# Down projection of a hybrid encoder block: PSUM banks from standing pools, another order of the pairs, and a block-wise end of the first column group

## The chip, the cores and the metric

One core of a Trainium2 chip runs the whole layer as one program. The metric is the device time of one execution in microseconds (us); runs of one kernel are compared by their median. TensorE (PE) does the matrix products, VectorE (DVE) and ScalarE (ACT) the elementwise work, SyncE (SP) issues the transfers.

## The reference, cut to what matters

A residual block on 256 tokens of width 2048 in float32: a normed input projection, eight heads of chunked attention and eight of a gated recurrence, an output projection, then the gated feed-forward part and a last norm. The change lies in the last product and what hangs on it:

```python
h2 = rmsnorm(x, norm2_gain[l])
ff = jax.nn.silu(h2 @ w_gate[l]) * (h2 @ w_up[l])      # 256 x 5632
x = x + (ff @ w_down[l]).astype(x.dtype)               # 5632 x 2048
return rmsnorm(x, final_gain)
```

## The kernel before, in words

**Split products.** Every float32 operand is split into a high and a low part (`split`, L86 to L88: ACT copies the rounded high part `wh`, DVE subtracts it from the source and gets `wl`), and a product is three matmuls: high by high, high by low, low by high. The weights stream through: `load_chunk` (L133) fetches 1 MB into one of three `raw` buffers, `halves_of` (L697) splits up to 1024 columns at a time into one of four `wh` and four `wl` buffers (`wsp`, L49).

**Gate and up.** The loop at L659 makes 22 blocks of 256 hidden columns. Each takes two banks of the pool `pacc` (four banks, tag `acc`) for the gate and two for the up product (`tr_product`, L159). `tr_evac` (L175) empties them: an ACT copy (L178), a DVE add that is the bank's last reader (L179), a DVE multiply (L180). The product of the two becomes `fh` and `fl`, the split hidden activations.

**Down.** The 5632 rows of `w_down` are 22 pairs of two 128-row blocks, the 2048 columns are two groups (g = 0, 1) of two 512-column halves. A group holds eight PSUM banks from the first product to the last: `c00`, `c01`, `c10`, `c11` (token half t, column half h) and `m1`, `m5`, `m6`, `m7`. A pair is done in one of two ways. *Ordinary* (`plain`, kind "d"): eight block products, 24 matmuls, for which DVE makes two 1024-column splits. *Seven-product* (`fast`, kind "s"): a Strassen-like scheme with seven block products, 21 matmuls, for which DVE makes three extra differences of the weights (`ta`, `tb`, L735 to L737) and splits 3.5 times 1024 columns. The seven-product pairs need sums of the activations, `sf`, made by four calls of `row_sums` (L679), each for two pairs. When the last seven-product pair of a group is done, `spread` (L767) adds the `m` banks into the residual `x2`; when the group is done, `add_res` (L782) adds the `c` banks, ACT takes the squares (L787), and DVE multiplies by the final gain (L788).

**Order of the work.** The lists `first` and `second` (L819 to L826) give the items in their order. Group 0: ordinary pairs 8 to 11, then pairs 0 to 7 as seven-product pairs, each followed by an ordinary one, then two ordinary ones: 8 seven-product and 14 ordinary pairs, 504 matmuls. Group 1 starts with a seven-product pair, has 504 matmuls too, and its last two pairs are kept (`tail`) and multiplied bank by bank, so that the closing norm (`finish`, L790) of one token half runs beside the products of the other. `row_sums` is called after items 1 to 4, `load_fg` (1 MB, the broadcast gain) after item 5. The banks of the down part come from a pool of their own, `pdn` (L675), opened after `pacc` and `paux` were closed (L668, L669). The scheduler of the framework keeps the program's dependencies but may place an engine's instructions a little earlier or later than they are written.

Of the kernel before, what the change touches and what calls it, by code (L numbers as in the profile page):

```python
# [8 lines left out]
F32 = mybir.dt.float32  # L9
# [19 lines left out]
FAST = 8  # L29
NT4 = 10  # L30
# [12 lines left out]
def hybrid_block(ctx: ExitStack, tc: tile.TileContext, x, xT, w_in, w_out, w_gu, w_down,  # L43
# [624 lines left out]
    auxs.__exit__(None, None, None)  # L668
    accs.__exit__(None, None, None)  # L669
# [5 lines left out]
    pdn = ctx.enter_context(tc.tile_pool(name="pdn", bufs=1, space=PSUM))  # L675
# [38 lines left out]
    class Group:  # L714
        def __init__(self, g, items):
            self.g, self.items = g, items
            self.bank = {n: pdn.tile([P, W], F32, tag=n, name=n) for n in
                         ("c00", "c01", "c10", "c11", "m1", "m5", "m6", "m7")}
            ns = sum(1 for kind, _ in items if kind == "s")
            nd = len(items) - ns  # L720
            self.left = {n: 3 * (ns + 2 * nd) if n in ("c00", "c01", "c10") else
                         6 * nd if n == "c11" else 3 * ns for n in self.bank}
            self.total = dict(self.left)

        def mul(self, n, lhs, rhs):
            for a, b in ((lhs[0], rhs[0]), (lhs[0], rhs[1]), (lhs[1], rhs[0])):
                nc.tensor.matmul(self.bank[n], lhsT=a, rhs=b, start=self.left[n] == self.total[n],  # L727
                                 stop=self.left[n] == 1)
                self.left[n] -= 1

        def fast(self, j):
            raw = load_pair(self.g, j)
            ta = dn.tile([P, 2, W], F32, tag="ta", name="ta")
            tb = dn.tile([P, 2, W], F32, tag="tb", name="tb")
            nc.vector.tensor_tensor(ta, raw[:, 1:3], raw[:, 0:2], ALU.subtract)  # L735
            nc.vector.tensor_tensor(tb[:, 0], raw[:, 2], ta[:, 0], ALU.subtract)
            nc.vector.tensor_tensor(tb[:, 1], raw[:, 3], tb[:, 0], ALU.subtract)  # L737
            b11, = halves_of(raw[:, 0:1])
            self.mul("m1", f_of(2 * j, 0), b11)
            t1, t3 = halves_of(ta)  # L740
            self.mul("m5", s_of(j, 0), t1)
            self.mul("m7", s_of(j, 2), t3)
            b22, b21 = halves_of(raw[:, 2:4])
            self.mul("c01", s_of(j, 3), b22)
            self.mul("c00", f_of(2 * j + 1, 0), b21)
            t2, t4_ = halves_of(tb)
            self.mul("m6", s_of(j, 1), t2)
            self.mul("c10", f_of(2 * j + 1, 1), t4_)

        def plain(self, j):  # L750
            raw = load_pair(self.g, j)
            out_ = []
# [5 lines left out]
        def plain_mul(self, steps, t=None, h=None):  # L758
            for k, hh, w in steps:
                for tt in range(NT):  # L760
                    if (t is None or tt == t) and (h is None or hh == h):
                        self.mul(f"c{tt}{hh}", f_of(k, tt), w)
# [19 lines left out]
    def add_res(gr, t, h):  # L782
# [4 lines left out]
        nc.scalar.activation(jk, x2[:, t, cols], AF.Square, accum_out=ss3[:, t, slot:slot + 1])  # L787
        nc.vector.tensor_tensor(x2[:, t, cols], x2[:, t, cols], fg[:, cols], ALU.mult)  # L788
# [28 lines left out]

    slow = list(range(FAST, KP))
    first = [("d", j) for j in slow[0:4]]  # L819
    later = slow[4:-2]  # L820
    second = []
    for i in range(FAST):
        first += [("s", i)] + [("d", j) for j in later[i:i + 1]]
        second += [("s", i)] + [("d", j) for j in slow[i:i + 1]]
    first += [("d", j) for j in slow[-2:]]
    second += [("d", j) for j in slow[FAST:]]  # L826
    sums = list(range(FAST // 2))
    for g, items in enumerate((first, second)):
        gr = Group(g, items)
        n_fast, tail = 0, []  # L830
        for n, (kind, j) in enumerate(items):
            if kind == "s":
                gr.fast(j)
                n_fast += 1
                if n_fast == FAST:
                    gr.spread()
            elif g == 1 and n >= len(items) - 2:
                tail += gr.plain(j)
            else:
                gr.plain_mul(gr.plain(j))  # L840
            if g == 0 and sums and (n >= 1):
                row_sums(sums.pop(0))
            if g == 0 and n == 5:
                load_fg()
        if g == 0:
            for t, h in ((0, 1), (0, 0), (1, 0), (1, 1)):
                add_res(gr, t, h)
        else:
            for t in range(NT):
                for h in range(2):  # L850
                    gr.plain_mul(tail, t, h)
                    if h == 0:
                        add_res(gr, t, h)
                finish(gr.bank[f"c{t}1"], t)
# [59 lines left out]
```

## Time and profile before

| | |
|---|---|
| three runs | 1174.12, 1174.25, 1175.63 us (median 1174.25) |
| the profiled execution | 1173.68 us, of which the span from first to last instruction is 1171.6 us |
| busy, share of the span | PE 99%, weight loads (PEld) 84%, DVE 70%, ACT 53% |
| down part, first and last matmul start | 928.94 and 1162.36 us |
| matmuls in the down part | 1008 |
| granted TensorE clock, mean | 0.998 |

How to read it: a row of a timeline is a start, a duration, the engine, the line, the operation, output<-inputs, and in brackets how long the engine had been idle and what ended that. A matmul's duration (0.39 us here) overlaps the next one's, so the spacing of starts, not the duration, is what a matmul costs in a stream. In the chain of waits a row gives start, length, and how many matmuls were merged (x27). A few records of matmuls are missing, so counts are taken from the code and not from the rows.

### The profile page before, as it was taken

The page shows a single profiled execution, that of the slowest core. Times are in us where ns is not written, and L with a number is a line of the kernel's source. Part 1 is how long each engine was busy: PE and PEld are TensorE (multiplying, and loading weights), DVE is VectorE, ACT ScalarE, POOL GpSimd, SP SyncE. Part 2 cuts the span into 40 slices and gives each one's busy share as a digit, 9 for nine tenths or more (in the row PEclk, how much of TensorE's full clock was granted, in tenths as well). Part 3 has the DMA queues.
Part 4 walks back from the last instruction along what each step waited for, and adds up shares of the span by engine and source line. Part 5 has one row for each costly group of instructions (what it writes and reads, how often), then busy time and mean ns, then how long its engine had stood idle before and what let it go on. Part 6 is the DMA issues. An engine that isn't in the chain of part 4 may idle for free.

```text
span 1171.6 us, 15526 instructions
## 1 busy us (share of the span) xinstructions
PE 1155.2 (99%) x6118; PEld 987.7 (84%) x6118; DVE 819.5 (70%) x1097; ACT 625.4 (53%) x858; POOL 19.1 (2%) x33
## 2 busy tenths in 40 slices
PE   9999999999999999999999999999999999999996
PEld 7888888888888888888888888888888777878885
DVE  7577778858646556666666657666666798899875
ACT  7465556747554455544445444444444455555543
POOL 3300000000000000000000000000000000000000
PEclk9999999999999999999999999999999999999999
DMA  8655454554745555555555555555555455656661
GB/s 313 240 206 193 145 180 168 193 179 146 279 151 180 180 180 180 185 204 187 182 193 201 180 185 200 191 180 193 201 182 184 175 181 214 216 180 216 212 219 72
DMA packets 35064, 223.85 MB, mean 191 GB/s; under 512 B 4144, under 2 KB 4656, under 8 KB 9520
## 3 DMA queue, kind: packets, MB, share of 16 engines
q1 hardware_dynamic: 34992, 222.87, 54.2%
q8 instruction: 48, 0.79, 0.3%
q14 instruction: 24, 0.20, 0.0%
HBM read 220.75 MB, written 2.10 MB: 190 GB/s over the span
## 4 chain that ended last, share of the span: by engine, by line
PE 93%; DVE 3%; DMA 1%; ACT 1%; issue 1%; SPq 0%; ACTq 0%; DVEq 0%
PE acc L168 38%; PE acc L170 19%; PE c L727 13%; PE acc L143 5%; PE acc L145 5%; PE acc L144 5%; PE m L727 3%; DVE wl L88 1%; PE vps L144 1%; PE vps L143 1%; PE vps L145 1%; DMA raw<-in_w_down_dram 1%; ACT wh L87 1%; DMA xr<-in_xT_dram 0%; PE pa L532 0%
## 5 line engine op out<-in xcount | busy, mean ns | idle before, releaser
L88 DVE TENSOR_TENSOR wl<-raw,wh 128x1024 fp32r<-128x1024 f32 (+1 forms) x418 | 492.8, 1184 | 276.6 <-ACT wh L87 271.7
L87 ACT ACTIVATE wh<-raw 128x1024 fp32r<-128x1024 f32 (+1 forms) x418 | 425.3, 1022 | 363.2 <-PE acc L168 215.5
L168 PE MATMUL acc<-h,wh 128*128 128x512 f32 x1408 | 488.6, 394 | 0.0
L170 PE MATMUL acc<-h,wl 128*128 128x256 f32 x1408 | 390.1, 277 | 0.0
L168 PEld LDWEIGHTS acc<-h,wh 128*128 128x128 f32 x1408 | 264.0, 188 | 61.4
L170 PEld LDWEIGHTS acc<-h,wl 128*128 128x128 f32 x1408 | 264.2, 188 | 0.0
L168 PE MATMUL acc<-hx,wh 128*128 128x512 f32 x512 | 179.7, 395 | 0.0
L170 PE MATMUL acc<-hx,wl 128*128 128x256 f32 x512 | 142.9, 279 | 0.0
L168 PEld LDWEIGHTS acc<-hx,wh 128*128 128x128 f32 x512 | 96.0, 187 | 21.5
L727 PE MATMUL c<-wh,fh 128*128 128x512 f32 x256 | 99.2, 391 | 3.1 <-DVE tb L179 2.7
L727 PE MATMUL c<-wl,fh 128*128 128x512 f32 x256 | 99.8, 390 | 0.1
L727 PE MATMUL c<-wh,fl 128*128 128x512 f32 x256 | 99.7, 389 | 0.0
L170 PEld LDWEIGHTS acc<-hx,wl 128*128 128x128 f32 x512 | 96.5, 189 | 0.1
L178 ACT COPY tb<-acc 128x256 f32<-128x256 f32 x120 | 43.3, 364 | 78.5 <-PE acc L170 78.5
L179 DVE TENSOR_TENSOR tb<-acc,tb 128x256 f32<-128x256 f32 x120 | 50.1, 421 | 30.3 <-ACT tb L178 30.3
L727 PEld LDWEIGHTS c<-wh,fh 128*128 128x128 f32 x256 | 47.9, 188 | 14.1 <-DVE tb L179 3.0
L727 PEld LDWEIGHTS c<-wl,fh 128*128 128x128 f32 x256 | 48.1, 188 | 10.9 <-DVE wl L88 0.9
L727 PEld LDWEIGHTS c<-wh,fl 128*128 128x128 f32 x256 | 48.1, 188 | 9.9
L143 PE MATMUL acc<-wh,hx 128*128 128x512 f32 x128 | 50.4, 394 | 0.0
L145 PE MATMUL acc<-wh,hx 128*128 128x512 f32 x128 | 49.9, 390 | 0.0
L144 PE MATMUL acc<-wl,hx 128*128 128x512 f32 x128 | 49.9, 389 | 0.0
L727 PE MATMUL m<-wh,sf 128*128 128x512 f32 x96 | 34.9, 391 | 0.6 <-ACT wh L87 0.6
(254 smaller groups left out, 1135.5 us busy)
## 6 DMA issues: line engine op xcount, KB each, us to landing
raw<-in_w_gu_dram SPq DMA_DIRECT2D x88, 1024.0 KB, 4.8
raw<-in_w_in_dram SPq DMA_DIRECT2D x48, 1024.0 KB, 4.9
raw<-in_w_down_dram SPq DMA_DIRECT2D x44, 1024.0 KB, 4.8
raw<-in_w_out_dram SPq DMA_DIRECT2D x16, 1024.0 KB, 4.8
raw<-in_w_in_dram SPq DMA_DIRECT2D x12, 512.0 KB, 6.7
raw<-in_w_in_dram SPq DMA_DIRECT2D x8, 256.0 KB, 5.0
x<-in_x_dram SPq DMA_DIRECT2D x2, 1024.0 KB, 9.3
out_dram<-x SPq DMA_DIRECT2D x8, 256.0 KB, 2.6
```

The lines of the kernel that those rows point to most:

```text
L87: nc.scalar.activation(hi, src, AF.Copy)
L88: nc.vector.tensor_tensor(lo, src, hi.bitcast(F32), ALU.subtract)
L143: nc.tensor.matmul(ps[t], lhsT=xh[:, tok], rhs=wh, start=kt == 0, stop=False)
L144: nc.tensor.matmul(ps[t], lhsT=xh[:, tok], rhs=wl, start=False, stop=False)
L145: nc.tensor.matmul(ps[t], lhsT=xl[:, tok], rhs=wh, start=False, stop=kt == kts - 1)
L168: nc.tensor.matmul(ps[m].rearrange("p j t -> p (j t)"), lhsT=wh[:, col], rhs=both, start=kt == 0, stop=False)
L170: nc.tensor.matmul(ps[m][:, 0, :], lhsT=wl[:, col], rhs=rhs[:, kt, 0, :], start=False, stop=kt == KD - 1)
L178: nc.scalar.copy(tb, ps[m][:, 1, :])
L179: nc.vector.tensor_tensor(tb, ps[m][:, 0, :], tb, ALU.add)
L727: nc.tensor.matmul(self.bank[n], lhsT=a, rhs=b, start=self.left[n] == self.total[n], stop=self.left[n] == 1)
```

## The change

Three things change, all in the down part.

1. **Banks.** `pacc` and `paux` stay open to the end. A group takes its eight banks from them, at its first product (`open`): the `c` banks in turn from `pacc`, the `m` banks from `paux`. The pool `pdn` is gone.
2. **Order and mix.** `order_of(fast, lead)` writes the lists. Group 0 now begins with six ordinary pairs (7 to 12) and has seven seven-product pairs (0 to 6); pair 7 becomes an ordinary one. Group 1 keeps eight, behind one ordinary pair. An ordinary pair now runs in the order c00, c01, c10, c11.
3. **Preparing and the group boundary.** `fast` and `plain` only load and split, and return their products as a list of steps; one loop over both groups prepares the next item and then multiplies. At the last pair of group 0 (`edge`) the first pair of group 1 is prepared first; the last pair is then multiplied bank by bank, `add_res` after each bank, and the four multiplications by the gain (`gained`) come after all of them.

The core of the diff:

```diff
-    accs = tc.tile_pool(name="pacc", bufs=4, space=PSUM)
-    pacc = accs.__enter__()
-    auxs = tc.tile_pool(name="paux", bufs=4, space=PSUM)
-    paux = auxs.__enter__()
+    pacc = ctx.enter_context(tc.tile_pool(name="pacc", bufs=4, space=PSUM))
+    paux = ctx.enter_context(tc.tile_pool(name="paux", bufs=4, space=PSUM))
...
-    auxs.__exit__(None, None, None)
-    accs.__exit__(None, None, None)
...
-    pdn = ctx.enter_context(tc.tile_pool(name="pdn", bufs=1, space=PSUM))
...
-            self.bank = {n: pdn.tile([P, W], F32, tag=n, name=n) for n in
-                         ("c00", "c01", "c10", "c11", "m1", "m5", "m6", "m7")}
+            self.bank = {}
...
+        def open(self):
+            for n in BANKS:
+                pool, tag = (pacc, "acc") if n[0] == "c" else (paux, "aux")
+                self.bank[n] = pool.tile([P, W], F32, tag=tag, name=n)
+
         def mul(self, n, lhs, rhs):
+            if not self.bank:
+                self.open()
...
-                out_ += [(2 * j + k, h if k == 0 else 1 - h, parts[h]) for h in range(2)]
-            return out_
+                steps += [(f"c{t}{h}", f_of(2 * j + k, t), parts[h if k == 0 else 1 - h])
+                          for t in range(NT) for h in range(2)]
+            return steps
...
+        def run_blocks(self, steps, blocks, after):
+            for t, h in blocks:
+                self.run([st for st in steps if st[0] == f"c{t}{h}"])
+                after(t, h)
...
+    def gained(gr, t, h):
+        cols = gr.cols(h)
         nc.vector.tensor_tensor(x2[:, t, cols], x2[:, t, cols], fg[:, cols], ALU.mult)
...
-    first = [("d", j) for j in slow[0:4]]
...
+    def order_of(fast, lead):
+        slow = [j for j in range(KP) if j not in fast]
+        items = [("d", j) for j in slow[:lead]]
+        mid = slow[lead:-2]
+        for n, j in enumerate(fast):
+            items += [("s", j)] + [("d", k) for k in mid[n:n + 1]]
+        return items + [("d", k) for k in mid[len(fast):]] + [("d", j) for j in slow[-2:]]
+
+    groups = [Group(0, order_of(list(range(FAST - 1)), 6))]
...
+    second = order_of(list(range(FAST)), 1)
...
-            for t, h in ((0, 1), (0, 0), (1, 0), (1, 1)):
-                add_res(gr, t, h)
...
+        if n == edge:
+            now, steps = steps, prepare(*todo[n + 1])
+            order = ((0, 0), (0, 1), (1, 0), (1, 1))
+            groups[0].run_blocks(now, order, lambda t, h: add_res(groups[0], t, h))
+            for t, h in order:
+                gained(groups[0], t, h)
+            continue
...
+        if n + 1 < len(todo):
+            steps = prepare(*todo[n + 1])
+    groups[1].run_blocks(held, ((0, 0), (0, 1), (1, 0), (1, 1)), last_block)
```

What this moves on the engines, at three places. Names carry a running number; the banks' names are those above, and all line numbers past the first lines shift (the matmul of `mul` is L727 before and L729 after).

**PE, first matmuls of the down part.** Before: the first rows; what stands in brackets are the engines or queues whose signals the instruction waits for.

```order
L727 MATMUL c00_8148<-wh_8158,fh_3829 128x512 [waits DMAHW4_49,DMAHW6_49,DMAHW2_49,DVE_49]
L727 MATMUL c00_8148<-wl_8159,fh_3829 128x512
L727 MATMUL c00_8148<-wh_8158,fl_3830 128x512
L727 MATMUL c10_8150<-wh_8158,fh_3829 128x512
L727 MATMUL c10_8150<-wl_8159,fh_3829 128x512
L727 MATMUL c10_8150<-wh_8158,fl_3830 128x512
L727 MATMUL c01_8149<-wh_8158,fh_3829 128x512
L727 MATMUL c01_8149<-wl_8159,fh_3829 128x512
L727 MATMUL c01_8149<-wh_8158,fl_3830 128x512
L727 MATMUL c11_8151<-wh_8158,fh_3829 128x512
```

After, from the fourth matmul on (three on `c00` from `wh_8145`, the first of which waits for ACT and the second for DVE, stand ahead of these):

```order
L729 MATMUL c01_8154<-wh_8145,fh_3829 128x512 [waits PE_49]
L729 MATMUL c01_8154<-wl_8146,fh_3829 128x512
L729 MATMUL c01_8154<-wh_8145,fl_3830 128x512
L729 MATMUL c10_8155<-wh_8145,fh_3829 128x512 [waits DVE_49]
L729 MATMUL c10_8155<-wl_8146,fh_3829 128x512
L729 MATMUL c10_8155<-wh_8145,fl_3830 128x512
L729 MATMUL c00_8153<-wh_8149,fh_3829 128x512
L729 MATMUL c00_8153<-wl_8150,fh_3829 128x512
L729 MATMUL c00_8153<-wh_8149,fl_3830 128x512
L729 MATMUL c11_8156<-wh_8145,fh_3829 128x512 [waits DVE_49]
L729 MATMUL c11_8156<-wl_8146,fh_3829 128x512
L729 MATMUL c11_8156<-wh_8145,fl_3830 128x512
```

Before, the first matmul on `c00` is the one that waits for DVE's reading of the old banks; after, the waits for DVE stand at the first matmul on `c10` and on `c11`, and `c11` has become the 13th matmul.

**DVE, around the first seven-product pair of group 0** (`a`, `sm`, `sf` are of `row_sums`; `ta`, `tb` of the seven-product pair). Before:

```order
L689 TENSOR_TENSOR sm_8311<-a_8310,sm_8311 128x256
L735 TENSOR_TENSOR ta_8321<-raw_8319 128x1024
L88 TENSOR_TENSOR sf_8146<-sm_8311,sf_8146 128x1024
L88 TENSOR_TENSOR wl_8334<-ta_8321,wh_8333 128x1024
L736 TENSOR_TENSOR tb_8322<-raw_8319,ta_8321 128x512
L88 TENSOR_TENSOR wl_8344<-raw_8319,wh_8343 128x1024
L737 TENSOR_TENSOR tb_8322<-raw_8319,tb_8322 128x512
L683 TENSOR_TENSOR a_8363<-fh_3829,fl_3830 128x1024
L88 TENSOR_TENSOR wl_8354<-tb_8322,wh_8353 128x1024
L88 TENSOR_TENSOR wl_8375<-raw_8372,wh_8374 128x1024
L686 TENSOR_TENSOR sm_8364<-a_8363 128x256
L688 TENSOR_TENSOR sm_8364<-a_8363 128x256
```

After:

```order
L684 TENSOR_TENSOR sm_8349<-a_8348 128x256
L683 TENSOR_TENSOR sm_8349<-sm_8349,a_8348 128x256
L685 TENSOR_TENSOR sm_8349<-a_8348,sm_8349 128x256
L737 TENSOR_TENSOR ta_8396<-raw_8394 128x1024
L87 TENSOR_TENSOR sf_8141<-sm_8349,sf_8141 128x1024
L87 TENSOR_TENSOR wl_8406<-ta_8396,wh_8405 128x1024
L738 TENSOR_TENSOR tb_8397<-raw_8394,ta_8396 128x512
L87 TENSOR_TENSOR wl_8410<-raw_8394,wh_8409 128x1024
L739 TENSOR_TENSOR tb_8397<-raw_8394,tb_8397 128x512
L737 TENSOR_TENSOR ta_8474<-raw_8472 128x1024
L87 TENSOR_TENSOR wl_8414<-tb_8397,wh_8413 128x1024
L87 TENSOR_TENSOR wl_8441<-raw_8438,wh_8440 128x1024
```

The fourth `row_sums` (here its `sm` rows) stood among the splits of the first seven-product pair and behind them, and stands ahead of that pair's differences now.

**DVE, at the boundary of the groups** (`x_2779` is the residual, `c_...` a bank, `fg` the gain). Before:

```order
L88 TENSOR_TENSOR wl<-ta,wh 128x1024
L735 TENSOR_TENSOR ta<-raw 128x1024
L784 TENSOR_TENSOR x_2779<-c_8149,x_2779 128x512
L784 TENSOR_TENSOR x_2779<-c_8151,x_2779 128x512
L784 TENSOR_TENSOR x_2779<-c_8148,x_2779 128x512
L788 TENSOR_TENSOR x_2779<-x_2779,fg 128x512
L784 TENSOR_TENSOR x_2779<-c_8150,x_2779 128x512
L88 TENSOR_TENSOR wl<-raw,wh 128x1024
L788 TENSOR_TENSOR x_2779<-x_2779,fg 128x512 x2
L88 TENSOR_TENSOR wl<-tb,wh 128x1024
L788 TENSOR_TENSOR x_2779<-x_2779,fg 128x512
```

After:

```order
L87 TENSOR_TENSOR wl<-raw,wh 128x1024
L737 TENSOR_TENSOR ta<-raw 128x1024
L738 TENSOR_TENSOR tb<-raw,ta 128x512
L87 TENSOR_TENSOR wl<-raw,wh 128x1024
L786 TENSOR_TENSOR x_2779<-c_8153,x_2779 128x512
L786 TENSOR_TENSOR x_2779<-c_8154,x_2779 128x512
L739 TENSOR_TENSOR tb<-raw,tb 128x512
L786 TENSOR_TENSOR x_2779<-c_8155,x_2779 128x512
L793 TENSOR_TENSOR x_2779<-x_2779,fg 128x512
L786 TENSOR_TENSOR x_2779<-c_8156,x_2779 128x512
L793 TENSOR_TENSOR x_2779<-x_2779,fg 128x512 x3
L87 TENSOR_TENSOR wl<-raw,wh 128x512
```

The additions from the four banks stood among the splits of a seven-product pair; now the splits of an ordinary pair are done ahead of them, and the splits of the first seven-product pair of group 1 follow the gain's multiplications.

More of the change, by code (lines that the diff above doesn't have):

```diff
@@ L29 @@
 FAST = 8
+BANKS = ("c00", "c01", "c10", "c11", "m1", "m5", "m6", "m7")
 NT4 = 10
@@ L721, in __init__ @@
             self.left = {n: 3 * (ns + 2 * nd) if n in ("c00", "c01", "c10") else
-                         6 * nd if n == "c11" else 3 * ns for n in self.bank}
+                         6 * nd if n == "c11" else 3 * ns for n in BANKS}
             self.total = dict(self.left)
+        def open(self):
+            for n in BANKS:
+                pool, tag = (pacc, "acc") if n[0] == "c" else (paux, "aux")
+                self.bank[n] = pool.tile([P, W], F32, tag=tag, name=n)
         def mul(self, n, lhs, rhs):
+            if not self.bank:
+                self.open()
             for a, b in ((lhs[0], rhs[0]), (lhs[0], rhs[1]), (lhs[1], rhs[0])):
@@ L738, in fast, with run @@
             b11, = halves_of(raw[:, 0:1])
-            self.mul("m1", f_of(2 * j, 0), b11)
             t1, t3 = halves_of(ta)
-            self.mul("m5", s_of(j, 0), t1)
-            self.mul("m7", s_of(j, 2), t3)
             b22, b21 = halves_of(raw[:, 2:4])
-            self.mul("c01", s_of(j, 3), b22)
-            self.mul("c00", f_of(2 * j + 1, 0), b21)
             t2, t4_ = halves_of(tb)
-            self.mul("m6", s_of(j, 1), t2)
-            self.mul("c10", f_of(2 * j + 1, 1), t4_)
+            return [("m1", f_of(2 * j, 0), b11), ("m5", s_of(j, 0), t1), ("m7", s_of(j, 2), t3),
+                    ("c01", s_of(j, 3), b22), ("c00", f_of(2 * j + 1, 0), b21),
+                    ("m6", s_of(j, 1), t2), ("c10", f_of(2 * j + 1, 1), t4_)]
         def plain(self, j):
             raw = load_pair(self.g, j)
-            out_ = []
+            steps = []
             for k in range(2):
                 parts = halves_of(raw[:, 2 * k:2 * k + 2])
-                out_ += [(2 * j + k, h if k == 0 else 1 - h, parts[h]) for h in range(2)]
-            return out_
[L758 to L762, printed above, removed]
+                steps += [(f"c{t}{h}", f_of(2 * j + k, t), parts[h if k == 0 else 1 - h])
+                          for t in range(NT) for h in range(2)]
+            return steps
+        def run(self, steps):
+            for st in steps:
+                self.mul(*st)
+        def run_blocks(self, steps, blocks, after):
+            for t, h in blocks:
+                self.run([st for st in steps if st[0] == f"c{t}{h}"])
+                after(t, h)
         def cols(self, h):
@@ L816, in finish @@
         dma(out[t, :, 1024:c0], x2[:, t, 1024:c0])
-    slow = list(range(FAST, KP))
-    first = [("d", j) for j in slow[0:4]]
[L820 to L826, printed above, removed]
-    sums = list(range(FAST // 2))
[L828 to L845, printed above, removed]
-            for t, h in ((0, 1), (0, 0), (1, 0), (1, 1)):
-                add_res(gr, t, h)
-        else:
[L849 to L854, printed above, removed]
@@ new lines, in hybrid_block, with prepare, last_block @@
+    todo += [(1, kind, j) for kind, j in second]
+    sums = list(range(FAST // 2))
+    n_fast, held = [0, 0], []
+    def prepare(g, kind, j):
+        if g == len(groups):
+            groups.append(Group(1, second))
+        return groups[g].fast(j) if kind == "s" else groups[g].plain(j)
+    def last_block(t, h):
+        if h == 0:
+            add_res(groups[1], t, h)
+            gained(groups[1], t, h)
+        else:
+            finish(groups[1].bank[f"c{t}{h}"], t)
+    edge = len(groups[0].items) - 1
@@ new lines, in hybrid_block @@
+    steps = prepare(*todo[0])
+    for n, (g, kind, j) in enumerate(todo):
+        if n == edge:
[5 more added lines that the diff above has]
+            continue
+        if n < len(todo) - 2:
+            groups[g].run(steps)
+        else:
+            held += steps
+        if kind == "s":
+            n_fast[g] += 1
+            if n_fast[g] == sum(1 for k, _ in groups[g].items if k == "s"):
+                groups[g].spread()
+        if sums and n >= 1:
+            row_sums(sums.pop(0))
+        if n == 5:
+            load_fg()
+        if n + 1 < len(todo):
+            steps = prepare(*todo[n + 1])
```

1 line of the change is left out of this document (added).

## The prediction

> **What bounds the kernel now.** I read the profile's page first, then the waits of PE in the down part, then the timeline where that part begins, then the chain of waits as a clock for it, and last VectorE (DVE) in the places where the clock loses time. The page's first lines:
>
> ```profile
> span 1171.6 us, 15526 instructions
> PE 1155.2 (99%) x6118; PEld 987.7 (84%) x6118; DVE 819.5 (70%) x1097; ACT 625.4 (53%) x858; POOL 19.1 (2%) x33
> ```
>
> PE is the bound, so only two things can move the time: fewer or more matmuls, and the places where PE stands still. The waits of PE from 920 us to the end (waited for, us in total, times, longest):
>
> ```profile
> PE c L727 <- DVE tb L179: 2.7, 1, 2.7
> PE m L727 <- DVE wl L88: 0.9, 2, 0.7
> PE m L727 <- ACT wh L87: 0.6, 1, 0.6
> PE c L727 <- ACT wh L87: 0.4, 2, 0.2
> PE c L727 <- DVE wl L88: 0.4, 1, 0.4
> ```
>
> That is 5.0 us, but these rows understate it: a matmul is shown for about 0.39 us while the next starts earlier, and that overlap is counted as work. So I use starts. The timeline where gate and up end and the down part begins:
>
> ```profile
> 921.78 1.23 DVE L88 TENSOR_TENSOR wl<-raw,wh 128x1024 fp32r<-128x1024 f32 x1 [1.61 <-ACT wh L87]
> ...
> 925.98 0.28 PE L170 MATMUL acc<-h,wl 128*128 128x256 f32 x1
> 926.35 0.42 DVE L179 TENSOR_TENSOR tb<-acc,tb 128x256 f32<-128x256 f32 x1 [0.58 <-ACT tb L178]
> ...
> 927.32 1.23 DVE L88 TENSOR_TENSOR wl<-raw,wh 128x1024 fp32r<-128x1024 f32 x1
> 928.47 0.42 DVE L179 TENSOR_TENSOR tb<-acc,tb 128x256 f32<-128x256 f32 x1
> 928.94 0.50 PE L727 MATMUL c<-wh,fh 128*128 128x512 f32 x1 [2.68 <-DVE tb L179]
> 929.28 0.39 PE L727 MATMUL c<-wl,fh 128*128 128x512 f32 x1
> 929.38 0.69 DVE L665 TENSOR_TENSOR ut<-ut,gt 128x512 f32<-128x512 f32 x1
> ```
>
> The last old matmul starts at 925.98, the first new one at 928.94, just behind the last reading of an old bank (928.47 + 0.42). The splits of the first pair were ready at 921.78 + 1.23 = 923.0. PE waits for banks alone. The stream also restarts with 0.34 instead of about 0.23 between two starts.
>
> The chain gives the rest as a clock (start, length, number of matmuls; a row m x9 opens a seven-product pair), and the last matmul is from the timeline:
>
> ```profile
> 995.21 2.04 PE m L727 x9
> 997.25 1.36 PE c L727 x6
> 998.61 0.68 PE m L727 x3
> 999.29 6.12 PE c L727 x27
> 1005.41 2.04 PE m L727 x9
> ...
> 1025.81 2.04 PE m L727 x9
> ...
> 1068.69 2.04 PE m L727 x9
> ...
> 1119.69 2.04 PE m L727 x9
> ```
>
> ```profile
> 1162.36 0.39 PE L727 MATMUL c<-wh,fl 128*128 128x512 f32 x1
> ```
>
> A seven-product pair and an ordinary one (21 + 24 = 45 matmuls) take 1005.41 - 995.21 = 10.20 us, 0.2267 us each. Now I count against that. The row at 995.21 is the fifth seven-product pair, behind 96 + 4 x 45 = 276 matmuls, or 62.6 us; 66.3 have passed since 928.94: 3.7 lost, 0.1 of it the restart. From 995.21 to 1025.81 are three periods exactly: nothing lost. From there 93 matmuls end group 0, and two periods of group 1 lead to 1068.69: 21.1 + 20.4 = 41.5 against 42.9, 1.4 lost at the boundary. From 1068.69 to 1119.69 nothing, and the last 188 (42.6) lose under 0.1. With 2.85 at the start (2.96 less a normal step of some 0.11, half of 0.2267 for a matmul with half the columns) the down part stands still for 8.0 us.
>
> Here the Trainium skill bears on the reading: its page "Perfetto Trace Analysis", section "Identifying the Most-Contended Engine", says that the busy share of matmuls is no good measure of the distance from the roofline. By the idle rows the change could win 5.0 - 0.7 = 4.3 us at most, by the starts 8.0 - 0.7 = 7.3; the trace's starts side with the page.
>
> **The change part by part.** The sum is made against the profiled execution's 1173.68 us (span 1171.6 and 2.1 around it); the median of the runs shown, 1174.25, lies 0.57 above it.
>
> *Three matmuls more.* Pair 7 of group 0 becomes ordinary: 24 - 21 = 3, times 0.2267: +0.7. The Trainium skill's "TensorE: Matmul & The Clock Gate", section "Back-to-back issue gap", gives about 131 ns for 512 columns in a sustained stream, which would make it +0.4; the rows say 227, and I take them.
>
> *Banks one by one.* `c00` and `c01` were the gate's banks, long read. The first matmul can start at 926.09, 2.85 earlier. `c10` is first used by the seventh matmul, at 926.09 + 6 x 0.2267 = 927.45, and was read by 926.77. `c11` is first used by the 13th, at 928.81, and its old reading (the add at 928.47, behind a split on DVE's queue) lets PE on at 928.94 as before: 0.13 lost, and the restart step stays. So -2.7. Were the order of banks not changed, the wait would come after nine matmuls, which would give -2.0; were the banks still waited for together, 0.
>
> *Six ordinary pairs first.* The rows of DVE before, in the stretch that loses 3.6 (3.7 less the restart):
>
> ```profile
> 950.52 0.69 DVE L736 TENSOR_TENSOR tb<-raw,ta 128x512 f32<-128x512 f32 x1
> 951.12 1.22 DVE L88 TENSOR_TENSOR wl<-raw,wh 128x1024 fp32r<-128x1024 f32 x1
> ...
> 954.13 1.23 DVE L88 TENSOR_TENSOR wl<-tb,wh 128x1024 fp32r<-128x1024 f32 x1
> 955.27 1.22 DVE L88 TENSOR_TENSOR wl<-raw,wh 128x1024 fp32r<-128x1024 f32 x1
> 956.41 0.42 DVE L686 TENSOR_TENSOR sm<-a 128x256 f32<-128x256 f32 x1
> 956.75 0.42 DVE L688 TENSOR_TENSOR sm<-a 128x256 f32<-128x256 f32 x1
> ```
>
> ```profile
> 929.90:951.00 21.10, 21.10 (x95) 17.46 (x94) 20.14 (x28) 12.29 (x14) 0.00 (x0) 1.00 0.50 196
> 951.00:990.00 39.00, 37.38 (x159) 28.94 (x158) 35.95 (x40) 21.87 (x24) 0.00 (x0) 1.00 0.54 189
> ```
>
> By the stretches (length, then busy PE, PEld, DVE, ACT, POOL, granted clock), DVE works 20.14 of 21.10 us: it is the engine that is late. From start to start 1024 columns cost 1.14, 512 cost 0.60, 256 cost 0.34. An ordinary pair is 2.3 of DVE for 5.44 of PE; a seven-product pair 4 x 1.14 (three splits and `ta`) + 3 x 0.60 = 6.4 for 4.76; a `row_sums` 2 x 1.14 + 4 x 0.34 and a little = 3.7. In the alternation DVE gains 10.2 - 8.7 = 1.5 per period, so a delay heals. After, by the order, DVE does from 929.38 (`ut`) to the last split of the first seven-product pair: `ut` and `fl` 1.4, eight splits of ordinary pairs 9.1, four `row_sums` 14.9, the pair itself 6.4, the next pair's `ta` 1.1: 33.0, plus about 0.8 of waiting for ACT's first copy, so the end is near 963.2. PE asks for that split at its 164th matmul: 926.09 + 0.24 + 163 x 0.2267 = 963.3. It is a draw; the two splits next to it, each asked for within five matmuls, come some tenths late. Carried row by row over all engines' queues, this count loses 0.8 after, and on before's order 2.7 where the trace has 3.6; scaled, 1.1. So 3.6 becomes 1.1: -2.5, with ends of -3.3 (all but 0.3 goes) and 0 (as late as before).
>
> *The boundary.* Before, DVE's additions and gain multiplications stand among the splits of a seven-product pair that PE wants at once:
>
> ```profile
> 1050.25 0.69 DVE L788 TENSOR_TENSOR x<-x,fg 128x512 f32<-128x512 f32 x1 [0.35 <-ACT jk L787]
> 1050.86 1.22 DVE L88 TENSOR_TENSOR wl<-tb,wh 128x1024 fp32r<-128x1024 f32 x1
> ...
> 1052.13 0.50 PE L727 MATMUL m<-wl,sf 128*128 128x512 f32 x1 [0.71 <-DVE wl L88]
> ```
>
> After, an ordinary pair stands there whose splits are done before the additions. Behind the last addition DVE owes three multiplications and the half split of the next pair: 5 x 0.60 = 3.0 at most, against 5.44 of PE cover. Each bank is read while the next one's six matmuls (1.36) run. Without that cover it would be the old 1.4. I take 0.1: -1.3.
>
> *At no cost:* the transfers keep their number and order (the gain's is still the seventh of the down part); a raw buffer comes free a little earlier. The closing blocks are in the same order, so the tail moves as a whole.
>
> Sum: +0.7 - 2.7 - 2.5 - 1.3 = -5.8, or 1167.9 in a profiled execution; with 0.57 the median is 1168.5. Ends: with every gain at its best +0.7 - 2.85 - 3.3 - 1.4 = -6.9 (1167.4); with the stall of the first pairs as long as before, -3.3 (1170.9).
>
> **The rivals.** *DVE gives the start back:* its work from 929.38 on does not move with PE's earlier start; if it is 2.5 us longer than I count, PE meets the first seven-product pair as late as before: -3.3, 1170.9. For it: the draw above; against: the row-by-row count errs by 0.9 on before. *The banks are still waited for together* (the change doesn't do what it says): PE starts at 928.94 as before, and DVE, with 2.7 us more cover, makes the early stall shrink to its best end: +0.7 - 3.3 - 1.3 = -3.9, 1170.3. Against it: after's order has DVE's signal at `c10` and `c11`. *No change to be measured:* the early stall stays and the boundary's 1.4 turns up at `m1` of the next pair: +0.7 - 2.7 = -2.0, 1172.2, within 0.2% of 1174.25 (2.35 us, about what a measurement of this kernel can tell from no change). *Slower, by the transfers:* a seven-product pair's weights are waited for already:
>
> ```profile
> DVE ta L735 <- DMA raw<-in_w_down_dram: 3.1, 3, 1.8
> ```
>
> ```profile
> 979.76 0.33 SPq L84 DMA_DIRECT2D raw<-in_w_down_dram  x1
> 985.92 1.23 DVE L735 TENSOR_TENSOR ta<-raw 128x1024 f32<-128x1024 f32 x1 [1.78 <-DMA raw<-in_w_down_dram]
> 988.33 0.50 PE L727 MATMUL m<-wl,sf 128*128 128x512 f32 x1 [0.21 <-DVE wl L88]
> ```
>
> Here 1 MB took from 979.76 to 985.9, 6.1 us, and behind the late `ta` the previous pair's split came late to PE. From some 6 us of landing on, each tenth is paid in every seven-product pair; were the new phase of the loads to make it 6.7, 15 pairs would pay 0.6 each (an estimate from these rows): 9.0 - 5.8 = +3.2, 1177.4. At 6.5 us on average (5.8 over 15 pairs is 0.4 each, above 6.1) the whole gain is gone. Against it: the alternation from 995.21 to 1025.81 lost nothing.
>
> **How the numbers follow.** Forecast 0.61, DVE gives the start back 0.17, banks together 0.06, no change 0.10, slower 0.06. The range 1167.0 to 1171.9 holds the forecast with its best end (0.4 below it for the runs' scatter) and the first two rivals; the last two and a little more are outside. Faster by over 0.2%: 0.61 + 0.17 + 0.06, less 0.03 for cases that fall just short, 0.81; same 0.10 + 0.03 = 0.13; slower 0.06.
>
> **What would show it.** In the profile after: the first matmul of the down part some 0.1 us behind the last of gate and up, and a short stop at the 13th; the first seven-product pair about 33 us later, with PE waiting for ACT or DVE by about 1 us in all around it; periods of 10.20; no wait at the boundary; the last matmul near 1156.6. The prediction is wrong if PE stands for 2 us or more at the first seven-product pairs, or if waits for transfers appear within the alternation.

## The result, and the profile after

The changed kernel takes 1167.88 us (median of four runs, 1167.05 to 1169.28). The kernel before took 1174.18 us on the same occasion (four runs, 1173.33 to 1175.63). The ratio is 0.9946, 95% interval 0.9929 to 0.9963: 6.3 us faster. The profiled execution after took 1168.06 us against 1173.68 before, 5.6 less. First the page of the kernel after, its span and the busy times:

```profile
span 1166.2 us, 15524 instructions
...
PE 1154.1 (99%) x6121; PEld 989.3 (85%) x6121; DVE 815.2 (70%) x1092; ACT 624.0 (54%) x856; POOL 19.0 (2%) x33
```

PE is busy 1.1 us less than before with three matmuls more, and the span is 5.4 shorter; the rest is idle time that went. The waits of PE from 920 us to the end (waited for, us in total, times, longest) had five rows and 5.0 us; now there are two:

```profile
PE m L729 <- DVE wl L87: 0.2, 1, 0.2
PE c L729 <- ACT wh L86: 0.2, 1, 0.2
```

The timeline of the kernel after where gate and up end:

```profile
925.91 0.28 PE L169 MATMUL acc<-h,wl 128*128 128x256 f32 x1
926.03 0.39 PE L729 MATMUL c<-wh,fh 128*128 128x512 f32 x1
...
928.41 0.41 DVE L178 TENSOR_TENSOR tb<-acc,tb 128x256 f32<-128x256 f32 x1
928.55 0.39 PE L729 MATMUL c<-wh,fl 128*128 128x512 f32 x1
928.88 0.50 PE L729 MATMUL c<-wh,fh 128*128 128x512 f32 x1
929.22 0.40 PE L729 MATMUL c<-wl,fh 128*128 128x512 f32 x1
929.32 0.69 DVE L664 TENSOR_TENSOR ut<-ut,gt 128x512 f32<-128x512 f32 x1
```

The first matmul of the down part now stands 0.12 behind the last of gate and up instead of 2.96. The 13th, the first on the last bank to be read, starts at 928.88, 0.33 behind the one ahead of it and not 0.23; the next follows in 0.34. So the start now costs 0.2.

The chain of waits after (start, length, what; a row m x9 opens a seven-product pair):

```profile
926.19 32.90 PE c L729 x144
959.09 2.04 PE m L729 x9
961.13 1.37 PE c L729 x6
...
962.53 1.01 ACT wh L86
...
970.23 2.04 PE m L729 x9
...
990.66 2.04 PE m L729 x9
...
1005.56 6.87 DMA raw<-in_w_down_dram
...
1013.66 1.23 DVE wl L87
...
1021.85 2.04 PE m L729 x9
...
1048.37 2.04 PE m L729 x9
...
1119.76 2.04 PE m L729 x9
```

Read it as a clock again, 0.2267 a matmul. From 959.09 to 970.23 are 11.14 us where a period is 10.20: 0.94 lost, at an ACT copy that came late because DVE's difference ahead of it did. From 990.66 to 1021.85 are 31.19 for three periods (30.60): 0.6 lost, behind a transfer of 6.87 us. From 1021.85 to 1048.37, over the boundary, are 26.52 for 117 matmuls: 26.52, nothing lost where 1.4 was. From there to 1119.76 are 71.39 for seven periods: nothing. The last matmul after starts 5.37 us earlier than it did:

```profile
1156.99 0.39 PE L729 MATMUL c<-wh,fl 128*128 128x512 f32 x1
```

### The profile page after: what moved, and what is told of

Same layout as the page of the kernel before. It is cut to its first block, busy times and chain, and to the rows that moved or that the text cites. A ratio compares the mean times of both kernels' runs of the same rounds, so it can differ in the third digit from the quotient of the medians.

```text
span 1166.2 us, 15524 instructions
## 1 busy us (share of the span) xinstructions
PE 1154.1 (99%) x6121; PEld 989.3 (85%) x6121; DVE 815.2 (70%) x1092; ACT 624.0 (54%) x856; POOL 19.0 (2%) x33
## 4 chain that ended last, share of the span: by engine, by line
PE 96%; DMA 1%; DVE 1%; ACT 1%; SPq 0%; issue 0%; ACTq 0%; DVEq 0%
PE acc L167 38%; PE acc L169 19%; PE c L729 15%; PE acc L142 5%; PE acc L144 5%; PE acc L143 5%; PE m L729 3%; PE vps L143 1%; PE vps L144 1%; PE vps L142 1%; DMA raw<-in_w_down_dram 1%; DMA raw<-in_w_in_dram 0%; DVE wl L87 0%; SPq L83 0%; PE pa L531 0%; PE po L550 0%
## 5 line engine op out<-in xcount | busy, mean ns | idle before, releaser
L729 PE MATMUL c<-wl,fh 128*128 128x512 f32 x262 | 102.2, 390 | 0.0
L729 PE MATMUL c<-wh,fh 128*128 128x512 f32 x262 | 102.0, 391 | 0.2 <-ACT wh L86 0.2
L729 PE MATMUL c<-wh,fl 128*128 128x512 f32 x262 | 102.1, 390 | 0.0
L729 PEld LDWEIGHTS c<-wh,fh 128*128 128x128 f32 x262 | 49.1, 188 | 11.2 <-ACT wh L86 0.6
L729 PEld LDWEIGHTS c<-wl,fh 128*128 128x128 f32 x262 | 49.2, 188 | 10.5 <-DVE wl L87 0.3
L729 PEld LDWEIGHTS c<-wh,fl 128*128 128x128 f32 x262 | 49.2, 188 | 10.1
L729 PE MATMUL m<-wh,sf 128*128 128x512 f32 x90 | 32.8, 391 | 0.1
```

## The experiments

**The theories.** *A, DVE's list is the clock:* DVE works through its instructions in order from about 929 us on, and that list decides when PE passes the first seven-product pairs, whenever PE began. Then the earlier banks gain nothing by themselves; the time comes only when the six ordinary pairs give DVE cover, which is work of PE that asks less of DVE than it lasts. *B, the terms add:* each part is worth its own stall wherever it is put, 2.7 for the banks and 2.5 for the order, as the sum of the prediction writes them. *C, the transfers:* what moves the time is how the loads of the weights fall. In the expectations, A and B are spelled out for each run.

All runs are in one table. "Length" is from the start of the last matmul of gate and up to the start of the last matmul of the program, in the profiled execution: it leaves out the part ahead, whose end lay between 925.33 and 927.09 us from kernel to kernel although nothing was changed there. The other columns are what PE lost at its stops against 0.2267 us a matmul (0.115 for the step behind the last matmul of gate and up, which has 256 columns): waiting for the banks (with the stop at the 13th matmul, where there is one, and the restarts), from 930 to 972 us, from 972 to 1030, at the boundary (1030 to 1060) and from there to 1140; they are good to about 0.03. Another 0.19 is lost near the end in all of them. The median in brackets is that of the kernel before, run on the same chip at the same time.

| kernel | median us (before) | ratio, 95% interval | length | banks | to 972 | to 1030 | boundary | to 1140 |
|---|---|---|---|---|---|---|---|---|
| before | 1174.25 | | 236.38 | 2.96 | 2.81 | 0.48 | 1.34 | 0 |
| after | 1167.88 (1174.18) | 0.9946 [0.9929, 0.9963] | 231.08 | 0.21 | 0.93 | 0.54 | 0 | 0 |
| banks_alone | 1173.89 (1174.35) | 0.9996 [0.9987, 1.0005] | 236.23 | 0.21 | 5.90 | 0 | 1.36 | 0 |
| six_first_alone | 1171.93 (1174.35) | 0.9979 [0.9969, 0.9989] | 234.35 | 2.96 | 0 | 0.64 | 1.35 | 0 |
| lead4 | 1172.93 (1174.35) | 0.9987 [0.9978, 0.9996] | 235.57 | 0.21 | 5.88 | 0 | 0 | 0 |
| joint_pool | 1170.37 (1174.35) | 0.9964 [0.9951, 0.9976] | 233.21 | 2.96 | 0 | 0 | 0 | 0.89 |
| old_edge | 1168.43 (1175.11) | 0.9942 [0.9929, 0.9956] | 233.37 | 0.21 | 0.89 | 1.46 | 1.30 | 0 |
| eight_fast | 1169.05 (1175.11) | 0.9954 [0.9940, 0.9969] | 231.71 | 0.21 | 0.94 | 0.09 | 1.67 | 0 |
| lead7 | 1167.74 (1175.11) | 0.9937 [0.9925, 0.9949] | 230.64 | 0.21 | 0 | 0 | 1.04 | 0 |
| late_sums | 1168.21 (1175.11) | 0.9940 [0.9928, 0.9953] | 230.62 | 0.21 | 0 | 1.03 | 0 | 0 |
| changed_again | 1167.74 (1174.37) | 0.9944 [0.9930, 0.9957] | 230.54 | 0.21 | 0.92 | 0 | 0 | 0 |
| extra_dve | 1170.11 (1174.37) | 0.9961 [0.9947, 0.9976] | 231.83 | 0.21 | 2.19 | 0 | 0 | 0 |
| lead7_edge2 | 1166.44 (1174.37) | 0.9931 [0.9918, 0.9945] | 229.57 | 0.21 | 0 | 0 | 0 | 0 |
| eight_edge3 | 1168.32 (1174.37) | 0.9945 [0.9931, 0.9959] | 229.95 | 0.21 | 0.90 | 0 | 0.10 | 0 |

**The banks alone.** The kernel before, with its order and its boundary, but with the banks of the down part from the standing pools:

```diff
-    pdn = ctx.enter_context(tc.tile_pool(name="pdn", bufs=1, space=PSUM))
...
-            self.bank = {n: pdn.tile([P, W], F32, tag=n, name=n) for n in
-                         ("c00", "c01", "c10", "c11", "m1", "m5", "m6", "m7")}
+            self.bank = {n: (pacc if n[0] == "c" else paux).tile(
+                [P, W], F32, tag="acc" if n[0] == "c" else "aux", name=n) for n in
+                ("c00", "c01", "c10", "c11", "m1", "m5", "m6", "m7")}
```

> The kernel before with one part of the change alone: the eight banks of a group come from the standing pools; lists, order and boundary as before. Theory A (DVE sets the pace: its work from 929.4 us on decides when PE gets past the first seven-product pairs, so an earlier start of PE is only waited out there): the first matmul of the down part comes 2.9 us earlier, the stops at the first two seven-product pairs grow from 3.6 to about 6.5 us, the last matmul starts within 0.7 us of before's 1162.36, and the time is that of before, 1174.2 within 1. Theory B (the parts add, as the prediction summed them): -2.7, some 1171.5, last matmul near 1159.7.

The ratio is 0.9996, interval 0.9987 to 1.0005: nothing that can be measured. Three rows of the timeline of the kernel before, stops of PE at the second seven-product pair:

```profile
964.93 0.50 PE L727 MATMUL c<-wl,sf 128*128 128x512 f32 x1 [0.39 <-DVE wl L88]
966.71 0.50 PE L727 MATMUL m<-wh,sf 128*128 128x512 f32 x1 [0.58 <-ACT wh L87]
967.66 0.73 PE L727 MATMUL c<-wh,fh 128*128 128x512 f32 x2 [0.22 <-ACT wh L87]
```

The same place with the banks alone, and two of the stops that are new at the first seven-product pair:

```profile
949.55 0.73 PE L723 MATMUL m<-wh,sf 128*128 128x512 f32 x2 [0.82 <-ACT wh L85]
...
952.54 0.50 PE L723 MATMUL c<-wl,sf 128*128 128x512 f32 x1 [0.38 <-DVE wl L86]
...
965.08 0.49 PE L723 MATMUL c<-wl,sf 128*128 128x512 f32 x1 [0.39 <-DVE wl L86]
966.85 0.51 PE L723 MATMUL m<-wh,sf 128*128 128x512 f32 x1 [0.58 <-ACT wh L85]
967.80 0.73 PE L723 MATMUL c<-wh,fh 128*128 128x512 f32 x2 [0.22 <-ACT wh L85]
```

PE began 3.08 us earlier (925.86 for 928.94) and passes this place 0.14 us later. The stops ahead of it have grown from 2.81 to 5.90, by 3.09. DVE's own clock has hardly moved: the last `ut` starts at 929.15 for 929.38, and the second `tb` of the first seven-product pair comes 23.26 us behind it for 22.88. That is A, to a few tenths; B, which gives 2.7 us, falls. The length is 0.15 shorter only because a transfer landed late in the kernel before (0.48) and none did here.

**Six ordinary pairs first, alone.** The kernel before with the order and the mix of the change (its three matmuls more, too), the banks still in the pool of their own and the boundary as it was:

```diff
-    first = [("d", j) for j in slow[0:4]]
-    later = slow[4:-2]
+    slow0 = list(range(FAST - 1, KP))
+    first = [("d", j) for j in slow0[0:6]]
+    later = slow0[6:-2]
...
-        first += [("s", i)] + [("d", j) for j in later[i:i + 1]]
+        if i < FAST - 1:
+            first += [("s", i)] + [("d", j) for j in later[i:i + 1]]
```

> The kernel before with the order and mix of group 0 alone: six ordinary pairs first, seven seven-product pairs; banks from a pool of their own, group 1 and the boundary as before. Theory A: PE starts at 928.9 as before, so DVE has 2.7 us more in hand than in the changed kernel, and the stops at the first seven-product pairs (3.6) vanish but for 0.3; with three matmuls more (+0.7) that is -2.6, 1171.6. Theory B: -2.5 + 0.7 = -1.8, 1172.4, with a stop of about 1.1 left.

1171.93 us, ratio 0.9979 [0.9969, 0.9989]. Its waits of PE:

```profile
PE c L727 <- DVE tb L179: 2.7, 1, 2.7
PE m L727 <- DVE wl L88: 1.1, 2, 0.7
```

The old 2.7 at the start is there, and no row of ACT: with a late start and six ordinary pairs the early stops are gone (0 of 2.81). The 1.1 is 0.4 behind a late transfer at 985 us and the 0.7 of the boundary. The length is 2.03 shorter: 2.81 less, 0.68 for the matmuls more, and 0.16 more behind the transfer make 1.97.

**The change with four ordinary pairs first.**

```diff
-    groups = [Group(0, order_of(list(range(FAST - 1)), 6))]
+    groups = [Group(0, order_of(list(range(FAST - 1)), 4))]
```

> The changed kernel with four ordinary pairs ahead of the first seven-product pair instead of six (the same pairs and number of matmuls). Theory A: the stops at the first two seven-product pairs are 5 to 6.5 us instead of 0.9, and the time 4.5 to 5.5 above the changed kernel, some 1172.9. Theory B: only the six-pair term goes, +2.5, some 1170.4.

1172.93 us, ratio 0.9987 [0.9978, 0.9996]: of the change's 6.3 us, 1.4 are left. Its waits of PE:

```profile
PE m L729 <- ACT wh L86: 2.0, 3, 0.8
PE c L729 <- DVE wl L87: 0.8, 2, 0.4
PE c L729 <- ACT wh L86: 0.6, 3, 0.2
```

All of them are early stops, 5.88 in all, as many as with the banks alone (5.90); the banks come early and the boundary costs nothing. Against the banks alone the length is 0.66 shorter, and the boundary's 1.36 less 0.68 for three matmuls makes 0.68. So nothing is left for the other things in which the two kernels differ, the order c00, c01, c10, c11 within an ordinary pair and the preparing of the next item, which no run tried by themselves.

**The change with a pool of its own for the banks.** Order and boundary as changed; the pools closed and `pdn` opened as before:

```diff
+    auxs.__exit__(None, None, None)
+    accs.__exit__(None, None, None)
...
+    pdn = ctx.enter_context(tc.tile_pool(name="pdn", bufs=1, space=PSUM))
...
-                pool, tag = (pacc, "acc") if n[0] == "c" else (paux, "aux")
-                self.bank[n] = pool.tile([P, W], F32, tag=tag, name=n)
+                self.bank[n] = pdn.tile([P, W], F32, tag=n, name=n)
```

> The changed kernel with the banks from a pool of their own again, opened when the old pools are closed; all else as changed. Theory A: PE starts 2.7 us later but the stop of 0.9 at the first seven-product pair goes, so the time is 1.8 above the changed kernel, some 1169.7. Theory B: 2.7 above it, some 1170.6, and the stop of 0.9 stays.

1170.37 us, ratio 0.9964 [0.9951, 0.9976]. The waits of PE are two:

```profile
PE c L733 <- DVE tb L180: 2.7, 1, 2.7
PE m L733 <- DVE wl L89: 0.6, 1, 0.6
```

The first is the start; the second lies at 1075 us in group 1, behind a transfer that landed late, 0.89 with its restart. Without that the length would be 232.32, and the change itself (230.54, without a late transfer) is 1.8 shorter. So the same edit of the banks is worth 0.15 of length ahead of four ordinary pairs (nothing without the late transfer of the kernel before) and 1.8 ahead of six: 2.7 of start less the 0.9 of stops that come back. The medians of different occasions give 0.9964 against 0.9946 and 0.9944, some 2 us, with intervals that overlap a little. Against six_first_alone, on the same chip, this kernel tells the boundary (with the order within a pair and the preparing): 1170.37 for 1171.93, 1.6 us less, with intervals that overlap, and 1.35 less at the boundary in the profile.

**The change with the old boundary.** Group 0 ends pair by pair, each `add_res` with its multiplication behind it, and group 1 begins with a seven-product pair:

```diff
-    second = order_of(list(range(FAST)), 1)
+    second = order_of(list(range(FAST)), 0)
...
-            now, steps = steps, prepare(*todo[n + 1])
-            order = ((0, 0), (0, 1), (1, 0), (1, 1))
-            groups[0].run_blocks(now, order, lambda t, h: add_res(groups[0], t, h))
-            for t, h in order:
+            groups[0].run(steps)
+            for t, h in ((0, 1), (0, 0), (1, 0), (1, 1)):
+                add_res(groups[0], t, h)
                 gained(groups[0], t, h)
+            steps = prepare(*todo[n + 1])
```

> The changed kernel with the old boundary of the groups: group 1 begins with its first seven-product pair, the last pair of group 0 is multiplied in the ordinary order, and the additions and gain multiplications come after it. Theory A: the additions stand among or ahead of the splits that PE wants next; counted along the queues, PE loses 0.3 to 0.7 there, so 0.5 above the changed kernel, some 1168.4. Theory B: the whole 1.3 comes back, some 1169.2, with a loss of 1.4 at the boundary.

The profile has the boundary's stops again, 1.30 us in all, as B expected. Its timeline:

```profile
1045.78 0.68 DVE L793 TENSOR_TENSOR x<-x,fg 128x512 f32<-128x512 f32 x1
1046.38 1.22 DVE L87 TENSOR_TENSOR wl<-raw,wh 128x1024 fp32r<-128x1024 f32 x1
...
1047.65 0.50 PE L729 MATMUL c<-wl,sf 128*128 128x512 f32 x1 [0.49 <-DVE wl L87]
```

The multiplication by the gain stands ahead of a split for which PE waits, as before. The same place of the kernel after has the additions and multiplications together, ahead of splits that PE doesn't ask for before 1048.37:

```profile
1043.04 0.68 DVE L786 TENSOR_TENSOR x<-c,x 128x512 f32<-128x512 f32 x1
1043.64 1.27 DVE L793 TENSOR_TENSOR x<-x,fg 128x512 f32<-128x512 f32 x2
...
1045.73 0.68 DVE L87 TENSOR_TENSOR wl<-raw,wh 128x512 fp32r<-128x512 f32 x1
1046.33 1.22 DVE L87 TENSOR_TENSOR wl<-ta,wh 128x1024 fp32r<-128x1024 f32 x1
```

The median does not show it. The profiled execution took 1170.54 us, with 1.46 lost behind a late transfer as well; the other four runs took 1168.12 to 1168.45, and the ratio, 0.9942, is no worse than the change's 0.9946 and 0.9944. So the boundary's 1.3 us is shown by the profiles, and joint_pool against six_first_alone leans the same way; the medians of this pair of kernels do not show it, and why stays open.

**Eight seven-product pairs in group 0 again.**

```diff
-    groups = [Group(0, order_of(list(range(FAST - 1)), 6))]
+    groups = [Group(0, order_of(list(range(FAST)), 6))]
```

> The changed kernel with eight seven-product pairs in group 0 again (three matmuls fewer), still behind six ordinary ones, so that the last two seven-product pairs have only two ordinary ones behind them. Theory A: DVE has no ordinary pairs left to recover on, with the second-last seven-product pair next to the last; the stops move to the boundary, about 2.5 us there, less 0.7 for the matmuls: 1.9 above the changed kernel, some 1169.8. Theory B (matmuls count, DVE recovers): 0.7 below it, some 1167.2.

1169.05 us, ratio 0.9954 [0.9940, 0.9969]. Three matmuls fewer save 0.68, and 1.67 is lost at the boundary: with eight, the alternation runs out of ordinary pairs between the last ones, and DVE's splits come late. With seven pairs, three more matmuls buy DVE the time to catch up there.

**Seven ordinary pairs first.** The same line with `7` for `6`.

> The changed kernel with seven ordinary pairs first in group 0 instead of six. Theory A: the stop of 0.9 at the first seven-product pair goes, but one ordinary pair fewer stands at the end, and 1.5 to 2.5 are lost at the boundary: 1 above the changed kernel, some 1168.9. Theory B: only the 0.9 goes, 0.9 below it, some 1167.0.

1167.74 us, ratio 0.9937 [0.9925, 0.9949]. The early stops are gone, in the chain from the first down matmul to the second pair without a row of any other engine:

```profile
926.17 38.34 PE c L729 x168
964.51 2.04 PE m L729 x9
...
974.71 2.04 PE m L729 x9
```

964.51 to 974.71 is 10.20. But 1.04 is lost at the boundary, where the change loses nothing, less than the 1.5 to 2.5 expected: the pair that went to the front is missing at the end. Cover is moved, not made, and the length (230.64) is that of the change without its late transfer (230.54).

**Sums of the activations later.** The fourth `row_sums` waits until the tenth item:

```diff
-        if sums and n >= 1:
+        if sums and (1 <= n <= 3 or n >= 9):
```

> The changed kernel with the fourth call of row_sums moved from behind the fifth item to behind the tenth, into the alternation. Theory A: the stop of 0.9 at the first seven-product pair goes, and one of about 0.8 comes where the moved sums are made, near 983 us: the time is that of the changed kernel within 0.5. Theory B: the stop goes and DVE's spare time in the alternation takes the sums for nothing: 0.9 below the changed kernel, some 1167.0.

1168.21 us, ratio 0.9940 [0.9928, 0.9953]. The early stops go (0 for 0.92), and 1.03 turns up at 983 to 985 us, behind the place to which the work was moved. The length is that of the change within 0.1.

**The change once more.** Unchanged, to be compared with the next three on the same chip.

> The changed kernel once more, so that the next three can be compared with it on one chip. All theories: 6 below the kernel before, some 1168, with 0.9 lost at the first seven-product pair and nothing at the boundary.

1167.74 us, ratio 0.9944 [0.9930, 0.9957]. In its profile no transfer is late, and the length is 230.54: 0.54 less than in the first profile of the same kernel, which is what the late transfer cost there.

**Three more DVE instructions.** Three additions of 512 columns, whose results nothing uses, written behind the fourth `row_sums` (in DVE's list they stand a little earlier, at 938.13, 944.28 and 948.63 us):

```diff
+        if n == 4:
+            for _ in range(3):
+                jk = dn.tile([P, W], F32, tag="jk", name="jk")
+                nc.vector.tensor_tensor(jk, x2[:, 0, 0:W], x2[:, 0, 0:W], ALU.add)
```

> The changed kernel with three additions of 512 columns put on DVE behind the fifth item of group 0 (results unused; 0.60 each by the rows before). Theory A (DVE's list decides when PE gets past the first seven-product pair): all 1.8 appear, the stops there go from 0.9 to 2.7, and the time is 1.8 above the changed kernel. Theory B (six ordinary pairs leave DVE room): nothing changes.

1170.11 us against 1167.74 on the same chip; the length is 1.29 longer. The timeline, DVE's second `tb` of the first seven-product pair and PE's stop for the copy made from it:

```profile
962.59 0.68 DVE L739 TENSOR_TENSOR tb<-raw,tb 128x512 f32<-128x512 f32 x1
...
964.50 0.50 PE L729 MATMUL m<-wh,sf 128*128 128x512 f32 x1 [0.57 <-ACT wh L86]
```

The last `ut` starts at 929.86 here, so the `tb` is 32.73 us behind it; in changed_again the two are at 929.24 and 960.68, 31.44. DVE's list is 1.29 longer, and PE is later by the same 1.29. That is less than the 1.8 (three times 0.60) that A named, and the stops reach 2.19 and not 2.7: in changed_again four rows of this stretch that write a buffer which the row just ahead of them reads start some 0.12 late (937.19 to 937.64 is 0.45 where 0.34 is usual); in extra_dve other rows stand in between, and these four delays are gone. The transfers are the same and none made PE stop: C does not explain it, A does. The median's 2.4 is more than the profile's 1.29 + 0.62, the last being the end of the part ahead.

**Seven ordinary pairs first, two at the head of group 1.**

```diff
-    groups = [Group(0, order_of(list(range(FAST - 1)), 6))]
+    groups = [Group(0, order_of(list(range(7)), 7))]
...
-    second = order_of(list(range(FAST)), 1)
+    second = order_of(list(range(FAST)), 2)
```

> The changed kernel with seven ordinary pairs first in group 0 and two instead of one at the start of group 1. Theory A: DVE gets its cover at both places; the 0.9 at the first seven-product pair and the 1.0 that the kernel with seven ordinary pairs first showed at the boundary both go, so it is 0.8 below the changed kernel, some 1167.1. Theory B (the loss at the boundary stays): the same as the changed kernel.

1166.44 us, ratio 0.9931 [0.9918, 0.9945], the fastest: 1.3 below the change on the same chip, with intervals that overlap. From 925 us to the end its waits of PE have no row at all. Its chain over the boundary:

```profile
1026.00 2.04 PE m L729 x9
...
1030.08 22.44 PE c L729 x99
1052.52 2.04 PE m L729 x9
...
1062.72 2.04 PE m L729 x9
```

From 1026.00 to 1052.52 are 26.52 for 117 matmuls, nothing lost, and the next period is 10.20. The only stops left are 0.2 at the 13th matmul and 0.19 near the end; 1011 matmuls without a stop would need 1010 x 0.2267 = 229.0 from the first to the last, and take 229.46.

**Eight seven-product pairs, three ordinary ones at the head of group 1.** `order_of(list(range(8)), 6)` and `order_of(list(range(FAST)), 3)`.

> The changed kernel with eight seven-product pairs in group 0 (three matmuls fewer) and three ordinary pairs at the start of group 1. Theory A: the 1.7 that eight seven-product pairs lost at the boundary go under the ordinary pairs, the 0.9 at the first seven-product pair stays, and the matmuls save 0.7: 0.7 below the changed kernel, some 1167.2. Theory B: the loss at the boundary stays and it is 1 above.

1168.32 us, ratio 0.9945 [0.9931, 0.9959]. The length is 0.59 below the change's (three matmuls fewer), so the boundary can be covered with eight as well (0.10 lost); the medians, 1168.32 and 1167.74, can't tell the two apart.

## Why the prediction was right, point by point

The forecast was 1168.5 and the median is 1167.88; in the profiled execution the sum gave -5.8 and the last matmul came 5.37 earlier. The profiled time fell by 5.62: 5.30 in the length, 0.07 ahead of it, and 0.25 behind the last matmul, which no term foresaw. So that the sum met the profiled time within 0.2 is in part luck.

*PE is the bound, counted by starts.* Right. By the idle rows the kernel before had 5.0 us to win, by the starts 8.0. lead7_edge2 won 6.81 of length while doing 0.68 more of matmuls, which is 7.5: more than the idle rows held. This bears out the sentence of the Trainium skill that the prediction named ("Perfetto Trace Analysis", section "Identifying the Most-Contended Engine").

*Three matmuls more, +0.7.* Right: eight_edge3 undoes them and is 0.59 shorter with 0.1 lost elsewhere. An estimate by the 131 ns of the Trainium skill's "TensorE: Matmul & The Clock Gate", section "Back-to-back issue gap", would be 0.4; the spacing stayed 227.

*Banks one by one, -2.7.* The size is right where it was put (2.96 to 0.21, the stop at the 13th matmul included). What was weak is that the sum wrote it as a term of its own: the six-pair term was counted with PE's earlier start in it, so the two together hold (-5.2 foretold, -4.6 measured), but not the split between them. Alone the banks are worth nothing (0.15 us of length, and that by another kernel's late transfer). The rival "DVE gives the start back" is no unlikely mishap but what happens in full with four ordinary pairs first (banks_alone and lead4); with six, 0.9 of it happens. The new order of the banks was not needed for it: the prediction gave -2.0 without that order, but banks_alone keeps the old order in its code and loses the same 0.21, at the 13th matmul too. The Trainium skill's "Perfetto Trace Analysis", section "Optimization Strategy", advises to find the gaps of the engine and let what blocks them complete sooner. Followed for the longest gap by itself, that gained nothing measurable here: 0.9996.

*Six ordinary pairs first, -2.5.* The term was mis-sized. It counted 3.6 us as DVE's, of which the stops from 930 to 972 are only 2.81; 0.48 was behind a transfer at 988 us, the chain's rows start 0.16 later than the timeline's (995.21 for 995.05), and the rest, 0.1, is steps a little longer than 0.2267. From 2.81 it fell to 0.93, so -1.9. The place and the reason (ACT's copy and DVE's split of the first seven-product pair, a draw between DVE and PE) are as foretold, and the 1.1 that should remain was 0.93.

*The boundary, -1.3.* 1.34 to 0 in the profile, and 1.30 again in old_edge's; by the medians it is not settled, as told there. It was foretold to be 0.1 and is 0.

*Transfers at no cost.* Right in number and order, wrong in that a single late landing can still cost something: 0.48 before, 0.54 after, 0.89 in joint_pool, 1.46 in old_edge, 0.64 in six_first_alone, and under 0.1 in the nine other profiles. This is the rival "slower by the transfers" in small: it hits one pair and not 15. The prediction had named a wait for a transfer within the alternation as a sign that it is wrong; the stop at 1014.9 us in the kernel after is one, so the sign was drawn too sharply. The 0.54 is most of what the first profile came out above the changed kernel's second one.

The terms as measured: -2.75 - 1.88 + 0.06 - 1.34 + 0.68 = -5.2, against -5.30 of length; 0.1 isn't found in the rows.

## What to carry to other kernels

Here a stall at the head of a stage was worth its length only where the engine that feeds the stage was ahead afterwards. So before crediting an earlier start, follow the feeding engine's in-order list to the first place where the two meet. Removing the wait and giving cover behind it are one change; either half alone gave 0.15 and 2.0 of 5.3 us here. Cover is a budget: a pair moved to the front was missing at the other end until a second one was put there.

## What the runs showed of the hardware that was not expected

A 1 MB load of weights mostly takes 4.8 us from issue to landing; those that made PE stop took 6 to 7. The view of the `raw` tiles in the kernel after, from 935 to 1150 us:

```profile
DMA to landing us min/median/max: 4.7/4.8/6.9
```

The DMA view of the same kernel, of the stretch with the late load, 1005 to 1013 us (queue and kind: packets, MB, share; then the issues):

```profile
q1 hardware_dynamic: 180, 1.34, 51.4%
q8 instruction: 1, 0.02, 1.0%
...
raw<-in_w_down_dram SPq DMA_DIRECT2D x2, 1024.0 KB, 5.8
```

There is one packet of another queue in it, named for instructions. The loads of that kernel that landed latest (issued at 940.09, 1005.56, 1034.69 and 1119.43 us: 6.1, 6.9, 6.1 and 5.8 us) all had such a packet inside, and so had those of old_edge at 940.42, 975.98, 1035.91 and 1122.24 (6.2, 7.1, 6.2 and 6.5). In the kernel before, in six_first_alone and in joint_pool the stretch ahead of the stop holds one too. In all 14 profiles, 574 loads of `w_down` were issued from 920 to 1150 us. Of the 50 with a packet of q8 wholly inside, 37 took 5.6 us or more, but 6 took less than 5.0; of the 83 that such a packet only touched at an edge, 3 took 5.6 or more; of the 441 without one, 2 did (one of them, 6.8 in old_edge, right behind the 7.1). That the packet delays the load is a reading of these counts and was not tried. It would explain why the late landing strikes another pair in each kernel. Most of the late loads made no stop of PE.

A stop of PE costs more than its idle time: behind nearly each of them the next matmul comes 0.34 us after the one that had waited, and not 0.23. So each stop has some 0.11 on top, and many short stops cost more than one of the same sum.
